# Transposes of the RMS norms' row sums moved to later places in the tensor engine's order at the borders of the MLP

## The chip, the cores and the metric

The kernel runs as one program on one core of a Trainium2 chip. The core has a tensor engine (PE, with its weight loads shown as PEld), a vector engine (DVE), a scalar engine (ACT), GpSimd (POOL) and a queue for transfers (SP). Each takes its own list of instructions in order, and semaphores tell one engine that another is done. The metric is the device time of one execution in microseconds, the median of several.

## The reference, cut to what matters

It is one step of a two-layer model over 1152 tokens (128 of context, 1024 latent), 1024 features wide. Every layer has a token mixer and an MLP, and an RMS norm stands ahead of each:

```
h = rmsnorm(x, P['norm1'][l]) * (1.0 + sc1) + sh1
mix, new_ctx = token_mixer(h, l, P, ctx)
x = x + g1 * mix
h = rmsnorm(x, P['norm2'][l]) * (1.0 + sc2) + sh2
u = jax.nn.relu(h @ P['w_mlp1'][l])
x = x + g2 * ((u * u) @ P['w_mlp2'][l])
```

`rmsnorm` divides each token's features by the root of their mean square.

## The kernel before, in words

**Layout.** Features lie on the 128 partitions and tokens along the free dimension. `x` is eight tiles (features 0 to 127, 128 to 255 and so on), written x0 to x7 below; the tokens are cut into three blocks of 384 (`tb` 0, 1, 2). Weights and activations are split into a high and a low part (`wh` and `wl`, `hh` and `hl`), and a product takes three matmuls of 128x384.

**The order.** The tensor engine's instructions stand exactly as the Python code issues them. For the other engines a scheduler makes the order when the program is built. Work that is to lie between matmuls is written as generators in `self.chain`; each call of `tick()` advances the first of them by one `yield`. In the MLP and in the input projections a tick comes after every 12 matmuls, in the output projection after every two steps of 6. I call 12 matmuls into one PSUM tile a group.

**A norm of one block** has these steps. `squares` (L305 to L311) squares the eight tiles on ACT and adds them up on DVE or POOL, ending in L311. After some empty ticks `rstd` transposes the sum on the tensor engine (L318, three transposes), reduces it over the features on DVE (L320, L321) and takes the power -1/2 on POOL (L323). `spread` copies the result to a full tile on DVE (L336), and one tick later transposes it back on the tensor engine (L341) and copies it out of PSUM on ACT (L343). Then `norm` makes `hh` and `hl` of the eight tiles, two to a tick: for most of them DVE multiplies (L355), ACT rounds (L356) and DVE takes the rest (L357), for the others POOL multiplies (L359), ACT scales and rounds (L361, L362) and DVE takes the rest (L363). All of these transposes use the one PSUM buffer of `pe`; L508 in the mixer, a transpose of a projection's result copied out by L510 on DVE, uses it too.

**Three borders.** The first is that between the output projection and the MLP of layer 0 (`norm2`), the third the same in layer 1. The output projection works on one block at a time, a group per tile of x, with two PSUM buffers (`pd`); each group is added to x on DVE (L1232) and so gives its buffer free. The weights of two groups come together, with a cast on ACT (L124) and a subtraction on DVE or POOL (L125). `chain` then holds the norms of the three blocks, and the first two row blocks of the MLP's first matrix (`up_unit`, 24 matmuls each) are made for block 0, then for block 1, then for block 2. What they leave is squared on ACT and POOL (L1266 to L1268) and split on DVE (L1269). The second border is that between the MLP of layer 0 and the projections of layer 1 (`norm1`): the last piece of the second matrix (`down_chunk`, added to x by L1290) is made block by block, with the norm of each block behind it.

## Time and profile before

| | us |
|---|---|
| median of 3 runs | 2906.37 (2906.33 to 2909.56) |
| the profiled execution's own time | 2915.1 |
| its span, first to last instruction | 2913.3 |
| busy in it: PE, DVE, ACT, POOL | 2750.3, 1457.1, 1119.5, 796.9 |

The profile is of one execution, whose times are a little longer than the median; differences are taken inside it. An engine's idle time costs something only where another engine, in the end the tensor engine, waits for it.

### The profile page before, as it was taken

The page shows a single profiled execution, that of the slowest core. Times are in us where ns is not written, and L with a number is a line of the kernel's source. Part 1 is how long each engine was busy: PE and PEld are TensorE (multiplying, and loading weights), DVE is VectorE, ACT ScalarE, POOL GpSimd, SP SyncE. Part 2 cuts the span into 40 slices and gives each one's busy share as a digit, 9 for nine tenths or more (in the row PEclk, how much of TensorE's full clock was granted, in tenths as well). Part 3 has the DMA queues.
Part 4 walks back from the last instruction along what each step waited for, and adds up shares of the span by engine and source line. Part 5 has one row for each costly group of instructions (what it writes and reads, how often), then busy time and mean ns, then how long its engine had stood idle before and what let it go on. Part 6 is the DMA issues. An engine that isn't in the chain of part 4 may idle for free. (4 is left out here: it accounts for less than half of the span.)

```text
span 2913.3 us, 41546 instructions
## 1 busy us (share of the span) xinstructions
PE 2750.3 (94%) x16067; PEld 2626.7 (90%) x16067; DVE 1457.1 (50%) x2577; ACT 1119.5 (38%) x2046; POOL 796.9 (27%) x848
## 2 busy tenths in 40 slices
PE   5898889999999999999988989899899999999998
PEld 4887887889999999999977879878899999999998
DVE  7645677795332333233475547868832333233235
ACT  4645447764112112211356436477622112211223
POOL 4233446642001001100223244576311001100112
PEclk7999999999999999999999999999999999999999
DMA  7545348321221111111343643662211111111113
GB/s 262 136 124 158 97 150 259 122 80 58 94 84 40 44 44 44 39 42 44 111 114 91 174 126 102 209 206 79 67 43 44 44 44 37 44 44 44 43 38 130
DMA packets 279301, 273.64 MB, mean 94 GB/s; under 512 B 30032, under 2 KB 259008, under 8 KB 279104
## 3 DMA queue, kind: packets, MB, share of 16 engines
q1 hardware_dynamic: 278888, 270.92, 30.5%
q8 instruction: 127, 2.08, 0.3%
q14 instruction: 70, 0.57, 0.1%
q10 hardware_dynamic: 216, 0.06, 0.0%
HBM read 227.02 MB, written 43.91 MB: 93 GB/s over the span
## 5 line engine op out<-in xcount | busy, mean ns | idle before, releaser
L161 PE MATMUL pg<-hh,wh 128*128 128x384 f32 x1856 | 634.6, 342 | 1.8 <-ACT hh L356 1.8
L162 PE MATMUL pg<-hl,wh 128*128 128x384 f32 x1856 | 630.3, 340 | 3.1 <-DVE hl L363 1.6
L163 PE MATMUL pg<-hh,wl 128*128 128x384 f32 x1856 | 629.5, 339 | 0.0
L124 ACT CAST wh<-wr 128x1024 fp32r<-128x1024 f32 x228 | 239.0, 1048 | 914.3 <-PE pg L162 878.7
L1268 POOL TENSOR_TENSOR te<-te 128x384 f32<-128x384 f32 x192 | 166.1, 865 | 1331.3 <-ACT uh L1267 1331.0
L163 PE MATMUL pg<-uh,wl 128*128 128x384 f32 x1536 | 514.1, 335 | 1.7 <-DVE wl L125 1.7
L161 PE MATMUL pg<-uh,wh 128*128 128x384 f32 x1536 | 515.0, 335 | 0.6 <-ACT wh L124 0.6
L162 PE MATMUL pg<-ul,wh 128*128 128x384 f32 x1536 | 513.8, 335 | 0.0
L1290 DVE SCALAR_TENSOR_TENSOR x<-pg,mod,x 128x384 f32<-128x384 f32 (+2 forms) x512 | 254.2, 515 | 395.7 <-PE pg L163 395.6
L161 PEld LDWEIGHTS pg<-hh,wh 128*128 128x128 f32 x1856 | 350.6, 189 | 8.6 <-issue 5.0
L162 PEld LDWEIGHTS pg<-hl,wh 128*128 128x128 f32 x1856 | 350.8, 189 | 6.1 <-DVE hl L363 3.1
L125 DVE TENSOR_TENSOR wl<-wr,wh 128x1024 fp32r<-128x1024 f32 x196 | 244.8, 1249 | 216.3 <-ACT wh L124 216.3
L163 PEld LDWEIGHTS pg<-hh,wl 128*128 128x128 f32 x1856 | 350.3, 189 | 0.0
L1269 DVE TENSOR_TENSOR ul<-te,uh 128x384 fp32r<-128x384 f32 x192 | 107.1, 558 | 452.0 <-POOL te L1268 452.0
L161 PEld LDWEIGHTS pg<-uh,wh 128*128 128x128 f32 x1536 | 288.5, 188 | 4.3 <-issue 1.7
L163 PEld LDWEIGHTS pg<-uh,wl 128*128 128x128 f32 x1536 | 288.5, 188 | 2.3 <-DVE wl L125 2.2
L162 PEld LDWEIGHTS pg<-ul,wh 128*128 128x128 f32 x1536 | 288.5, 188 | 0.0
L1266 ACT ACTIVATE te<-pg 128x384 f32<-128x384 f32 x192 | 93.8, 489 | 358.5 <-PE pg L163 358.5
L161 PE MATMUL pd<-hh,wh 128*128 128x384 f32 x544 | 198.8, 366 | 7.8 <-DVE te L558 3.6
L162 PE MATMUL pd<-hl,wh 128*128 128x384 f32 x544 | 192.2, 353 | 3.4 <-DVE hl L397 3.4
L163 PE MATMUL pd<-hh,wl 128*128 128x384 f32 x544 | 191.4, 352 | 0.0
L1225 PE MATMUL pd<-mh,wh 128*128 128x384 f32 x384 | 137.2, 357 | 13.3 <-DVE x L1232 13.3
(293 smaller groups left out, 4216.4 us busy)
## 6 DMA issues: line engine op xcount, KB each, us to landing
wr<-in_w_mlp_dram SPq DMA_DIRECT2D x144, 512.0 KB, 4.0
wm<-in_w_mod_dram SPq DMA_DIRECT2D x96, 512.0 KB, 4.9
wr<-in_w_out_dram SPq DMA_DIRECT2D x48, 512.0 KB, 4.6
wr<-in_w_in_dram SPq DMA_DIRECT2D x36, 512.0 KB, 5.3
xd<-x SPq DMA_DIRECT2D x48, 192.0 KB, 3.8
x<-xd SPq DMA_DIRECT2D x48, 192.0 KB, 4.3
raw<-mixd SPq DMA_DIRECT2D x40, 192.0 KB, 3.0
B<-gkd SPq DMA_DIRECT2D x16, 288.0 KB, 4.7
```

Of the source, the lines that this page charges most:

```text
L124: nc.scalar.copy(hi[:, :m], raw[:, :m])
L125: lo_eng.tensor_tensor(lo[:, :m], raw[:, :m], f32(hi[:, :m]), ALU.subtract)
L161: mm(out, wh[i], xs[i][0], start=i == 0, stop=False)
L162: mm(out, wh[i], xs[i][1], start=False, stop=False)
L163: mm(out, wl[i], xs[i][0], start=False, stop=i == n - 1)
L1225: nc.tensor.matmul(p[:, :TB], wh[:, k, sl], xs[k][0], start=k == 0, stop=False)
L1266: nc.scalar.activation(r, p[:, :TB], AF.Relu)
L1268: nc.gpsimd.tensor_tensor(r, r, r, ALU.mult)
L1269: nc.vector.tensor_tensor(blk(ul, tb), r, f32(blk(uh, tb)), ALU.subtract)
L1290: nc.vector.scalar_tensor_tensor(xa, p[:, a:b], self.M[l]["g2"][:, dt, s:s + 1], xa, ALU.mult, ALU.add)
```

## The change

It gives `norm_rs` and `spread` a number of empty ticks (`slack`) and sets it by block and border. At the first and third border the spread of block 0 gets one more empty tick, the sum of block 1 one more, and block 2's sum has its squares issued at once, in tiles of the pool `te`, while its transposes queue behind the norm of block 1 and not ahead of the norm of block 0. At the second border block 0's spread gets one more tick, and block 2's sum has four empty ticks and not two. No instruction is added or removed.

```diff
-    def norm_rs(self, x, tb, ret, alloc=None, eng0=None):
+    def norm_rs(self, x, tb, ret, alloc=None, eng0=None, slack=2):
         acc = self.squares(x, tb, alloc, eng0)
-        for _ in range(2):
+        for _ in range(slack):
             yield
         ret[tb] = self.rstd(acc)
         yield
 
-    def spread(self, rs, tile):
+    def spread(self, rs, tile, slack=1):
...
-        for _ in range(1):
+        for _ in range(slack):
             yield
...
-        pbs = yield from self.spread(ret[tb], tile)
+        pbs = yield from self.spread(ret[tb], tile, 1 if tb else 2)
...
-                    self.chain.insert(0, self.norm_rs(self.xa, 1, self.rs2, eng0=nc.vector))
+                    self.chain.insert(0, self.norm_rs(self.xa, 1, self.rs2, eng0=nc.vector, slack=3))
...
-            self.chain.insert(0, self.norm_rs(self.xa, 2, self.rs2, eng0=nc.vector))
+            rs2 = self.norm_rs(self.xa, 2, self.rs2, self.te, nc.vector, slack=1)
+            next(rs2)
+            self.add(rs2)
             norm2(2)
...
-                self.add(self.norm_rs(self.xa, tb, self.rs1))
+                self.add(self.norm_rs(self.xa, tb, self.rs1, slack=2 if tb < 2 else 4))
```

Between the transposes the tensor engine's list has these numbers of other matmuls. First and third border: L318 of block 0, then 24 to its L341 (now 36), 96 to L318 of block 1 (96), 36 to its L341 (48), 60 to L318 of block 2 (48), 24 to its L341 (24); the MLP's first matmul stands 24 behind L341 of block 1 before, and right behind it now. Second border: 24 (now 36), 108 (108), 24 (24), then 72 to L318 of block 2 with L508 among them (84), and 24 to its L341 (none but another L508).

The scheduler moves the other engines' instructions with them. On DVE, at the first border where the norm of block 0 begins (x_3702 to x_3709 are x0 to x7), the difference is this:

```order
 L1232 SCALAR_TENSOR_TENSOR x_3703<-pd,mod_1_2797,x_3703 128x384
 L1232 SCALAR_TENSOR_TENSOR x_3704<-pd,mod_1_2797,x_3704 128x384
+L1232 SCALAR_TENSOR_TENSOR x_3705<-pd,mod_1_2797,x_3705 128x384
 L355 SCALAR_TENSOR_TENSOR tn<-x_3702,G_5516,tn 128x128
 L355 SCALAR_TENSOR_TENSOR tn<-x_3702,G_5516,tn 128x256
```

The addition for x3 has moved ahead of the norm's first multiplication, as the matmuls of x3 have ahead of L341. On ACT the copy L343 stands likewise behind one more L124, and on POOL the multiplications L359 behind one more L125.

On DVE at the same border, where the sum of block 2 is reduced (L320), the list before is this, from the end of its squares (L311):

```order
L311 TENSOR_TENSOR tn<-tn 128x384
L1269 TENSOR_TENSOR ul<-te,uh 128x384
L363 TENSOR_TENSOR hl_6220<-tn,hh_6212 128x384
L320 TENSOR_REDUCE ms<-pe 128x3
L357 SCALAR_TENSOR_TENSOR hl_6221<-tn,mod_1_2797,hh_6213 128x384
```

And now:

```order
L311 TENSOR_TENSOR te<-te 128x384
L363 TENSOR_TENSOR hl_6218<-tn,hh_6210 128x384
L357 SCALAR_TENSOR_TENSOR hl_6219<-tn,mod_1_2797,hh_6211 128x384
L1269 TENSOR_TENSOR ul<-te,uh 128x384
L363 TENSOR_TENSOR hl_6220<-tn,hh_6212 128x384
L357 SCALAR_TENSOR_TENSOR hl_6221<-tn,mod_1_2797,hh_6213 128x384
L355 SCALAR_TENSOR_TENSOR tn<-x_3708,G_5516,tn 128x384
L355 SCALAR_TENSOR_TENSOR tn<-x_3709,G_5516,tn 128x384
L1269 TENSOR_TENSOR ul<-te,uh 128x384
L363 TENSOR_TENSOR hl_6222<-tn,hh_6214 128x384
L357 SCALAR_TENSOR_TENSOR hl_6223<-tn,mod_1_2797,hh_6215 128x384
L357 SCALAR_TENSOR_TENSOR hl_6224<-tn,mod_1_2797,hh_6216 128x384
```

hl_6217 to hl_6224 are the low parts of tiles 0 to 7, here all of block 1, and L320 is the row behind the last of these. Between L311 and L320 stood two instructions, and now stand eleven, up to the end of block 1's norm.

On the tensor engine at the second border, around the transposes of block 2, the difference is this:

```order
 L162 MATMUL pg<-hl_12731,wh 128x384
 L163 MATMUL pg<-hh_12723,wl 128x384
+L318 MATMUL pe<-ident,tn 128x128 x3
+L508 MATMUL pe<-ident,te 128x128 x3
 L341 MATMUL pe<-ident,tn 128x128 x3
-L508 MATMUL pe<-ident,te 128x128 x3
 L161 MATMUL pg<-hh_12716,wh 128x384
```

L318 has come down by 24 matmuls and now stands, with only L508 between, ahead of the L341 that needs its result.

## Rows read from the trace of the kernel before

**Rows 1.** Busy time by stretch (us, busy and count by engine, PE clock, DMA)

```profile
612.50:678.40 65.90, 56.58 (x319) 53.73 (x319) 61.71 (x101) 41.03 (x80) 24.66 (x20) 1.00 0.23 72
678.40:1445.00 766.60, 766.60 (x4401) 757.83 (x4400) 254.38 (x438) 162.94 (x260) 83.13 (x95) 1.00 0.19 58
1445.00:1509.00 64.00, 54.26 (x293) 51.47 (x292) 53.60 (x85) 36.55 (x72) 21.22 (x20) 0.95 0.37 113
2036.90:2102.70 65.80, 58.30 (x313) 55.81 (x313) 60.20 (x100) 40.94 (x80) 24.03 (x20) 0.95 0.24 72
```

**Rows 2.** PE's waits in the first border: total us, times, longest

```profile
PE pe L318 <- DVE tn L311: 4.8, 2, 3.0
PE pd L1225 <- DVE x L1232: 3.4, 2, 1.8
```

**Rows 3.** PE's waits in the second border

```profile
PE pe L318 <- DVE tn L311: 4.0, 2, 3.0
...
PE pg L163 <- DVE wl L125: 1.7, 1, 1.7
...
PE pe L508 <- ACT tn L343: 0.6, 1, 0.6
```

**Rows 4.** PE's waits in the third border

```profile
PE pe L318 <- DVE tn L311: 4.7, 2, 3.0
```

**Rows 5.** PE in order of time, first border: start, us, instruction, [idle before]

```profile
617.21 0.49 PE L341 MATMUL pe<-ident,tn 128*128 128x128 f32 x3
619.51 0.44 PE L1225 MATMUL pd<-mh,wh 128*128 128x384 f32 x1 [1.82 <-DVE x L1232]
...
627.63 0.41 PE L1225 MATMUL pd<-mh,wh 128*128 128x384 f32 x1 [1.60 <-DVE x L1232]
...
660.83 0.52 PE L318 MATMUL pe<-ident,tn 128*128 128x128 f32 x3 [3.01 <-DVE tn L311]
...
665.64 0.52 PE L341 MATMUL pe<-ident,tn 128*128 128x128 f32 x3
```

**Rows 6.** DVE in order of time, first border

```profile
616.51 2.42 DVE L1202 TENSOR_TENSOR ml<-oraw,mh 128x128 fp32r<-128x128 f32 x1
...
619.90 1.66 DVE L355 SCALAR_TENSOR_TENSOR tn<-x,G,tn 128x128 f32<-128x128 f32 x3
...
626.88 0.60 DVE L1232 SCALAR_TENSOR_TENSOR x<-pd,mod,x 128x384 f32<-128x384 f32 x1
...
659.34 1.35 DVE L311 TENSOR_TENSOR tn<-tn 128x384 f32<-128x384 f32 x1
...
662.35 0.55 DVE L320 TENSOR_REDUCE ms<-pe 128x3 f32<-128x384 f32 x1
...
676.78 1.18 DVE L357 SCALAR_TENSOR_TENSOR hl<-tn,mod,hh 128x384 fp32r<-128x384 f32 x1
```

**Rows 7.** POOL in order of time, first border

```profile
616.42 2.36 POOL L125 TENSOR_TENSOR wl<-wr,wh 128x1024 fp32r<-128x1024 f32 x1
618.74 2.01 POOL L359 TENSOR_TENSOR tn<-x,tn 128x384 f32<-128x384 f32 x2
```

**Rows 8.** ACT in order of time, first border

```profile
615.30 1.05 ACT L124 CAST wh<-wr 128x1024 fp32r<-128x1024 f32 x1
617.73 0.48 ACT L343 COPY tn<-pe 128x384 f32<-128x384 f32 x1 [1.39 <-PE pe L341]
```

**Rows 9.** PE in order of time, second border

```profile
1494.15 0.52 PE L318 MATMUL pe<-ident,tn 128*128 128x128 f32 x3 [2.98 <-DVE tn L311]
...
1500.26 0.49 PE L341 MATMUL pe<-ident,tn 128*128 128x128 f32 x3
```

**Rows 10.** DVE in order of time, second border

```profile
1494.70 0.56 DVE L320 TENSOR_REDUCE ms<-pe 128x3 f32<-128x384 f32 x1 [0.70 <-PE pe L318]
...
1496.43 0.55 DVE L336 COPY tn<-rs 128x384 f32<-128x384 f32 x1 [0.97 <-POOL rs L323]
```

**Rows 11.** Busy time by stretch, behind the second border's longest wait

```profile
1495.40:1498.80 3.40, 3.40 (x12) 3.40 (x12) 0.61 (x2) 0.00 (x0) 0.86 (x1) 0.50 0.02 5
```

## The prediction

> **What bounds the kernel now.** I read the busy time by stretch first. In the stretch of the first MLP the tensor engine is busy for all of its 766.6 us, 4401 matmuls at 0.174 us each; the second MLP runs the same code. In the three borders it is not: 9.3 of 65.9 us are idle in the first, 9.7 of 64.0 in the second, 7.5 of 65.8 in the third [rows 1]. Nothing after a border then has slack to take up a delay, so a microsecond won or lost in a border is one in the total. All that this change can win lies in those 26.5 us.
>
> Then the waits, border by border. The transposes of the sums (L318) wait for the end of the squares (L311) on DVE: 4.8 us in two waits in the first border, 4.0 in the second, 4.7 in the third, the longest of each 3.0, which is that of block 2 [rows 2, 3, 4]. The other waits are on DVE as well, or on the scalar engine behind it. DVE itself is busy for 61.7 of the 65.9 us of the first border [rows 1]. The reader should keep this number: the tensor engine waits there because DVE has no time left, and a matmul order that only moves a wait gives DVE none. What helps is only what spares DVE idle time; what costs is what makes it idle.
>
> **The change part by part.** Twelve matmuls take 2.1 us and 24 take 4.2. I go through the first border and sum up what becomes later.
>
> *Block 0's L341 behind one more group.* Before, it ran at 617.21, and then the tensor engine waited 1.82 us, until 619.51, for the addition of x1, which frees a PSUM buffer [rows 5]. That addition is late because a DVE subtraction of 616.51 took 2.42 us, ending as POOL's weight subtraction of 616.42 (2.36 us) ends [rows 6, 7]. Neither is touched, so the third group still cannot start before 619.5. It ends at 621.7; only then L341 runs, outside any wait: 0.4 us that were free. The copy to SBUF (L343, 0.48 us, at 617.73 before) now stands behind a second weight cast of 1.05 us, which waits for the same group since it overwrites its weights [rows 8]: 621.7 + 1.05 + 0.5 gives 623.2. DVE's first multiplication of block 0 was at 619.90 [rows 6], so it is 3.3 us late, and DVE has only the addition for x3 to do meanwhile. From that first multiplication to the addition for x4 DVE took 7.0 us, 619.90 to 626.88 [rows 6], and the next group, at 627.63, waited 1.60 us for it [rows 5]. In the new order four instructions have left this path (x3's addition, two pieces for x4, one low part), estimated at 1.7 us together from three multiplications that took 1.66 us beside POOL [rows 6]. So x4 comes at 623.2 + 7.0 - 1.7 = 628.5 and not 626.9: **1.6 us later**. It could be 0, if the rest of the list gives it back, or 2.5, if POOL's multiplications, two in 2.01 us [rows 7], all fall on DVE's.
>
> This last point is a rule too. The rows show that DVE's subtraction of two SBUF tiles ends only when POOL's does, while additions that read PSUM ran beside POOL. The Trainium skill, "SBUF — State Buffer", section "Who interferes with whom", says that a DVE instruction with two SBUF inputs and a GpSimd instruction that reads SBUF exclude each other for the whole instruction. By the rule alone, with three more POOL multiplications of 1.0 us falling on DVE's in each outer border, the sum below would be 6 us greater; the trace agrees with the lock, but how the two meet in the new order no row shows.
>
> *Block 1's L318, 12 matmuls later.* Its wait was 1.8 us (4.8 less 3.0) [rows 2]; 2.1 us of matmuls now run ahead of it, but the squares inherit part of the delay above. I take **1.2 us won**, between 0.6 and 1.8.
>
> *Block 2's L318, 12 matmuls later, its squares issued at once.* The wait was 3.0 us [rows 5]. DVE now does three instructions of block 1's norm among these squares that it had done before (0.5 us each), with one more POOL multiplication beside them. I take **1.5 us won**, between 0.5 and 3.0.
>
> *Block 2's reduction (L320) behind all of block 1's norm on DVE.* Before, it began 1.7 us after L311's end at 660.7, at 662.35, and L341 followed 3.3 us later, at 665.64 [rows 5, 6]. During that time DVE worked on block 1. Now eleven instructions stand between L311 and L320. At some 0.5 us each and one POOL square of 1.0 us that is 6.6 us. From L320 to the end of the copy L336 it takes 2.3 us at least: 1494.70 to 1496.98, in the second border where nothing stands between [rows 10]. So L341 comes 8.9 us after L311, against 5.0. The tensor engine has L318 and 24 matmuls to do in it, 4.6 us, both before and now. It is kept waiting for the rest, partly by block 1's last low parts, partly by L341 itself, behind which the ready unit of block 1 queues: **4.2 us lost** (2.5 to 5).
>
> *Block 2's norm.* From L341 to its last low part, 665.64 to 677.96, were 12.3 us [rows 5, 6], in which the tensor engine had 36 matmuls and then most of the unit that reads them, 10.6 us: 1.7 late. Now L341 is 24 matmuls ahead, so 8.5 us, and the chain is 11.2, two low parts of block 1 (1.1 us) having gone out of it: 2.7 late, **1.0 us lost** (0 to 2). In this time DVE has also lost cover: while L323, L336, L341 and L343 pass the sum along, it has one low part of the MLP to do.
>
> The first border sums to 1.6 + 0.4 - 1.2 - 1.5 + 4.2 + 1.0 = **4.5 us lost**; as the parts share causes I hold 0 to 7 possible. The third border has the same order and the same two waits at L318 [rows 4]: another **4.5 us**, 0 to 7.
>
> *Second border.* L318 of block 2 moves 24 matmuls down, so its 3.0 us wait goes [rows 3]. But L341 now follows with only L508 between. From L318's start to the copy's end were 2.8 us, 1494.15 to 1496.98 [rows 9, 10]; the single PSUM buffer of `pe` must also be emptied of L508's result first (0.5). Less 0.8 for the two sets of transposes 2.6 us come back. The 24 matmuls took 5.6 us, from 1494.67 to 1500.26 [rows 9], since the engine's clock was granted at half (1.2 GHz) from 1495.4 to 1498.8, after the wait [rows 11]; now they run ahead of any wait, 1.4 us less. I leave a like slow stretch behind the new wait, 1.3 us. L508's 0.6 us behind L341 goes, block 1's 1.0 us at L318 goes, and the weight waits (1.7 at the low part [rows 3]) move on to the next pair of weights, which now stands behind the norm: 0.6 us more. Sum: -3.0 + 2.6 - 1.4 + 1.3 - 0.6 - 1.0 + 0.6 = **1.5 us won**, between 4 won and 1 lost.
>
> Together 4.5 + 4.5 - 1.5 = 7.5 us lost. The profiled execution took 2915.1 us and would take 2922.6; it stands 8.7 us above the median of 2906.4, to which I carry the difference: **2914 us**.
>
> **The rivals.** *The waits at L318 go and nothing comes back* (faster). All of 4.8 + 4.0 + 4.7 = 13.5 us [rows 2, 3, 4] would be won: 2893. Its point is the reduction: if in the outer borders L320 of block 2 runs early enough for L341 to come within the 4.6 us of matmuls behind L318, the 4.2 us term vanishes. For it speaks that L318's are the largest group of waits; against it that L320 stands behind eleven instructions and DVE's list is taken in order. Anything from 2893 to 2900 would be this case.
>
> *It balances* (within 0.2%, which is 5.8 us and about what a measurement of this kernel can tell from no change). If DVE's instructions meet fewer of POOL's than I think, the front costs nothing and the tail 2.5, not 4.2: an outer border then sums to 0 + 0.4 - 1.5 - 2.2 + 2.5 + 1.0 = 0.2, the total to -1, 2905. DVE's work is the same before and after, which speaks for it; the idle time that it gets while the copy is on its way speaks against.
>
> *The clock falls in all borders.* The new waits come close together (the one at x4, block 1's low parts, L341, block 2's low parts). A half-rate stretch like that of 1495.4, in which 12 matmuls began in 3.4 us [rows 11], against 20 at 0.174, costs 1.3 us. Two more in each outer border would give 2914 + 5 = 2919. For it speaks the 0.95 of the second and third border; against it that the first had 9.3 us of waits and kept 1.00 [rows 1], and that a slow tensor engine costs nothing while DVE is late. The Trainium skill, "TensorE: Matmul & The Clock Gate", section "What's actually happening", has the clock halve when the engine has been idle and rise after it has been kept busy; the second border agrees.
>
> **How the numbers follow.** My forecast, 5.8 to 11 us lost, gets 0.43; the clock's case, beyond that, 0.12; balance 0.33; the faster case 0.12. So slower 0.55, same 0.33, faster 0.12. The likeliest's own range is 2912 to 2917. For 8 in 10 I go from 2903, which leaves out the faster case and a little of balance, to 2923, both borders near their upper bound.
>
> **What the profile after would show.** Right: the first border's wait at L318 shrinks from 4.8 to about 3; a wait of about 2 us stands before block 2's L341, where none was; the group after x4's addition starts 1 to 2.5 us later, seen from block 0's L318; L162 waits in the units of blocks 1 and 2 for low parts, some 4 us together; the two outer borders each take about 70 us, not 66; in the second L318 does not wait and L341 does, for 2 to 3 us. Wrong: if L320 of block 2 is not late on DVE, the 4.2 us are wrong; if the outer borders take 66 us or less, so is the sum. The forecast fails as well if DVE's busy time in a border shrinks by several us, because POOL and DVE meet less often than before.

## The result, and the profile after

The change makes the kernel slower: 2923.81 us (median of 4 runs, 2921.97 to 2925.34) against 2907.97 us beside it (2906.33 to 2911.37). The ratio is 1.0053, with an interval of 1.0035 to 1.0070, which is 15.4 us (10 to 20). The direction of the forecast was right and its size was half: 7.5 us. The time lies just above 2923, the upper end of the range that was to hold in 8 cases of 10.

The two profiled executions cannot be compared by their spans (2913.3 and 2921.1 us). Ahead of the first border, where both run the same instructions, the one before lost 6.75 us more. So I measure from one L318 of block 0 to the next. The tensor engine in order of time, before (the last row is the first L318 of the final norm):

```profile
612.62 0.55 PE L318 MATMUL pe<-ident,tn 128*128 128x128 f32 x3
1445.44 0.49 PE L318 MATMUL pe<-ident,tn 128*128 128x128 f32 x3
2037.03 0.44 PE L318 MATMUL pe<-ident,tn 128*128 128x128 f32 x2
2864.20 0.49 PE L318 MATMUL pe<-ident,tn 128*128 128x128 f32 x3
```

And after:

```profile
605.87 0.44 PE L318 MATMUL pe<-ident,tn 128*128 128x128 f32 x2
1445.32 0.49 PE L318 MATMUL pe<-ident,tn 128*128 128x128 f32 x3
2039.14 0.44 PE L318 MATMUL pe<-ident,tn 128*128 128x128 f32 x2
2872.05 0.49 PE L318 MATMUL pe<-ident,tn 128*128 128x128 f32 x3
```

The first border with its MLP took 832.82 us and takes 839.45; the third 827.17 and 832.91. Between them lies a mixer whose length varies, so for the second border I compare matmul by matmul: the 300th behind L318, where the border is over, comes 3.07 us later than before. Busy time by stretch, the three borders after, answering to [rows 1]:

```profile
605.75:678.30 72.55, 60.08 (x319) 56.06 (x319) 62.69 (x101) 41.45 (x80) 23.96 (x20) 0.95 0.22 65
...
1444.90:1511.90 67.00, 56.67 (x296) 53.21 (x294) 55.73 (x87) 37.34 (x72) 24.88 (x23) 0.90 0.36 109
2039.00:2110.60 71.60, 59.44 (x314) 55.39 (x313) 61.82 (x100) 41.36 (x80) 23.95 (x20) 0.95 0.22 66
```

The same 319 matmuls stand in 72.55 us and not 65.90. Of the 6.65 us more, 3.15 are idle time of the tensor engine and 3.50 are busy time (60.08 less 56.58): the granted clock is 0.95 and was 1.00, so some of the same matmuls ran at half rate. DVE's work in the stretch is nearly the same, 62.7 us against 61.7. The waits of the first border, answering to [rows 2]:

```profile
PE pd L1225 <- DVE x L1232: 4.9, 2, 2.7
PE pg L162 <- DVE hl L363: 2.7, 3, 1.2
PE pe L318 <- DVE te L311: 1.8, 1, 1.8
PE pe L341 <- DVE tn L336: 1.7, 1, 1.7
PE pg L162 <- DVE hl L357: 1.4, 2, 0.9
```

L318 lost 3.0 of its 4.8 us, as the change intends. In their place stand 1.7 at L341, 4.1 at low parts (L162), where 1.1 stood, and 1.5 more at x's additions. The second border, answering to [rows 3]:

```profile
PE pg L163 <- DVE wl L125: 4.0, 2, 3.4
PE pg L161 <- ACT hh L356: 2.9, 1, 2.9
PE pe L341 <- DVE te L510: 1.6, 1, 1.6
```

Its 4.0 us at L318 are gone altogether, and 4.0 stand at the weights' low parts, where 1.7 stood, 2.9 at `hh`, where 1.8 stood, and 1.6 at block 2's L341. The tensor engine at the front of the first border, answering to [rows 5]:

```profile
612.75 0.45 PE L1225 MATMUL pd<-mh,wh 128*128 128x384 f32 x1 [2.17 <-DVE x L1232]
616.38 0.62 PE L341 MATMUL pe<-ident,tn 128*128 128x128 f32 x3
623.90 0.66 PE L1225 MATMUL pd<-mh,wh 128*128 128x384 f32 x1 [2.72 <-DVE x L1232]
```

DVE there and at block 2's reduction, answering to [rows 6]:

```profile
616.62 0.62 DVE L1232 SCALAR_TENSOR_TENSOR x<-pd,mod,x 128x384 f32<-128x384 f32 x1 [3.40 <-PE pd L1227]
617.93 4.25 DVE L355 SCALAR_TENSOR_TENSOR tn<-x,G,tn 128x128 f32<-128x128 f32 x3 [0.69 <-ACT tn L343]
...
655.82 1.35 DVE L311 TENSOR_TENSOR te<-te 128x384 f32<-128x384 f32 x1
...
663.89 0.54 DVE L320 TENSOR_REDUCE ms<-pe 128x3 f32<-128x384 f32 x1
```

And POOL at the front, answering to [rows 7]:

```profile
617.47 2.39 POOL L125 TENSOR_TENSOR wl<-wr,wh 128x1024 fp32r<-128x1024 f32 x1 [5.45 <-ACT wh L124]
619.82 2.21 POOL L359 TENSOR_TENSOR tn<-x,tn 128x384 f32<-128x384 f32 x2
```

DVE waits 3.40 us for the tensor engine, which works on the group ahead of L341. Its first three multiplications then take 4.25 us (1.66 before) and end at 622.18, as POOL's do at 622.03. L320 runs 6.7 us behind the end of L311 (663.89 less 657.17), where 6.6 had been worked out.

### The profile page after: what moved, and what is told of

The parts are those of the page before. It is cut to its first block, busy times and chain, and to the rows that moved or that the text cites. A ratio compares the mean times of both kernels' runs of the same rounds, so it can differ in the third digit from the quotient of the medians.

```text
span 2921.1 us, 41549 instructions
## 1 busy us (share of the span) xinstructions
PE 2755.6 (94%) x16067; PEld 2628.1 (90%) x16067; DVE 1458.9 (50%) x2577; ACT 1120.5 (38%) x2046; POOL 798.2 (27%) x848
## 5 line engine op out<-in xcount | busy, mean ns | idle before, releaser
L162 PE MATMUL pg<-hl,wh 128*128 128x384 f32 x1856 | 630.9, 340 | 9.9 <-DVE hl L363 5.9
L124 ACT CAST wh<-wr 128x1024 fp32r<-128x1024 f32 x228 | 239.0, 1048 | 932.0 <-PE pg L162 880.9
L162 PE MATMUL pg<-ul,wh 128*128 128x384 f32 x1536 | 514.1, 335 | 0.0
L162 PEld LDWEIGHTS pg<-hl,wh 128*128 128x128 f32 x1856 | 350.0, 189 | 16.4 <-DVE hl L363 8.9
L125 DVE TENSOR_TENSOR wl<-wr,wh 128x1024 fp32r<-128x1024 f32 x196 | 245.4, 1252 | 219.0 <-ACT wh L124 219.0
L162 PEld LDWEIGHTS pg<-ul,wh 128*128 128x128 f32 x1536 | 289.0, 188 | 0.0
L162 PE MATMUL pd<-hl,wh 128*128 128x384 f32 x544 | 191.8, 353 | 3.4 <-DVE hl L397 3.4
```

What stands on the lines that cost most here:

```text
L124: nc.scalar.copy(hi[:, :m], raw[:, :m])
L125: lo_eng.tensor_tensor(lo[:, :m], raw[:, :m], f32(hi[:, :m]), ALU.subtract)
L162: mm(out, wh[i], xs[i][1], start=False, stop=False)
```

## The experiments

All runs in one table: the ratio to the kernel before; the distance from L318 to L318 for the first and the third border (us); and how much later than before the 300th matmul behind the second border's L318 comes. Where a border's code is unchanged, the traces spread by themselves: 832.8 to 834.7, 826.1 to 827.2, and 0 to 1.7 (mean 1.1). A border's cost is read against the means 833.5, 826.6 and 1.1 of the unchanged ones. What makes the spread is told under "The half-rate stretches".

| kernel | ratio (95%) | first | third | second |
|---|---|---|---|---|
| before | | 832.82 | 827.17 | 0 |
| the change | 1.0053 (1.0035 to 1.0070) | 839.45 | 832.91 | 3.07 |
| 1: block 0's L341 later, outer | 1.0030 (1.0019 to 1.0042) | 837.61 | 830.07 | 1.49 |
| 2: block 1's sum later, outer | 0.9992 (0.9983 to 1.0001) | 832.41 | 825.80 | 0.03 |
| 3: block 2's sum, outer | 1.0022 (1.0013 to 1.0031) | 837.53 | 830.89 | 0.77 |
| 4: block 0's L341 later, second | 1.0013 (1.0004 to 1.0022) | 832.83 | 826.12 | 3.68 |
| 5: block 2's sum later, second | 0.9999 (0.9990 to 1.0009) | 834.73 | 827.11 | 0.07 |
| 4, weights asked for early | 1.0022 (1.0013 to 1.0031) | 833.48 | 826.12 | 5.77 |
| change, block 2's sum inserted | 1.0060 (1.0045 to 1.0075) | 841.15 | 832.31 | 3.01 |
| change, wait filled | 1.0041 (1.0027 to 1.0055) | 838.30 | 833.94 | 3.41 |
| 1 and 4, copy on DVE | 1.0049 (1.0033 to 1.0064) | 836.68 | 831.06 | 4.94 |
| 1 and 4, ticks kept | 1.0055 (1.0042 to 1.0069) | 838.14 | 832.36 | 4.63 |
| 2, wait filled | 0.9993 (0.9985 to 1.0002) | 832.15 | 825.43 | 1.34 |
| 2 in all borders | 0.9997 (0.9988 to 1.0006) | 832.51 | 825.62 | 1.10 |
| before, less on DVE | 0.9972 (0.9959 to 0.9984) | 829.10 | 822.48 | 1.72 |
| change, less on DVE | 1.0034 (1.0021 to 1.0046) | 836.12 | 829.59 | 2.35 |
| before, weights by DVE | 0.9991 (0.9981 to 1.0000) | 831.64 | 824.30 | 1.43 |
| 1, weights by DVE | 1.0014 (1.0004 to 1.0024) | 834.72 | 829.06 | 1.73 |
| change, weights by DVE | 1.0029 (1.0018 to 1.0040) | 833.98 | 828.28 | 3.05 |

### Single parts

Each part of the change alone, on the kernel before. The edits 1 and 4 give `norm` the number of empty ticks, at the outer borders or at the second:

```diff
-        pbs = yield from self.spread(ret[tb], tile)
+        pbs = yield from self.spread(ret[tb], tile, slack)
...
+                                        lambda kt, b: blk(hl[kt], b), slack=1 if tb else 2))
...
+                         lambda kt, b: blk(self.hl1[kt], b), lambda: self.spill(tb), slack=1 if tb else 2)
```

The other edits are lines of the change: 2 `slack=3` for block 1's sum, 3 the three lines of `rs2`, 5 `slack=2 if tb < 2 else 4`.

> One part alone: in the outer borders block 0's L341 stands 12 matmuls later, all else as before. If the front is late because its copy L343 and DVE's first multiplication come later (my term, which measured 3.0 us in the changed kernel), each outer border is 2 to 4 us longer, seen from one L318 of block 0 to the next, and the time 4 to 8 us above the kernel before. If DVE makes good the delay before the sum of block 1 is wanted, the wait at block 1's L318 shrinks and the time is within 2 us of before. If it is the clock that made the front dear, the border is longer by 1.3 us for each half-rate stretch that appears and by no more.

> One part alone: in the outer borders block 1's L318 stands 12 matmuls later. Before, it waited 1.8 us for DVE and block 2's L318 waited 3.0. My term has 1.2 us won per outer border, 2.4 in all. If DVE alone sets the time, the wait is only handed on: none is left at block 1's L318, that of block 2 grows to 4 to 5 us, and the time is within 1 us of before. If the waits of the sums are a cost by themselves, 3.6 us are won.

> One part alone: in the outer borders block 2's squares are issued at once and its L318 queues behind the norm of block 1. My terms: 1.5 us won at L318, 4.2 lost because L320 stands behind block 1's norm on DVE, 1.0 lost in block 2's own norm, so 3.7 per outer border and 7.4 in all. If the wait at L318 goes and nothing comes back, 3 us are won per border. If the front and not the tail carries the loss, it is within 2 us of before.

> One part alone: in the second border block 0's L341 stands 12 matmuls later. In the changed kernel the first wait for the low part of the weights (L163 behind L125) was 3.4 us where 1.7 and 0.6 had been forecast together, and a half-rate stretch of 6.8 us stood around it. If this part puts L125 on DVE behind more of the norm, the wait is 2.5 to 3.5 us here too and the second border 1.5 to 4 us longer. If the later place of block 2's sum does it, the wait stays at 1.7 and the border within 0.5 us.

> One part alone: in the second border the sum of block 2 has four empty ticks and not two, so that L318 stands 24 matmuls later and L341 right behind it. My terms: the 3.0 us at L318 go, 2.6 come back at L508 and L341, 1.4 us of half-rate matmuls go, 1.3 come again behind the new wait, L508's 0.6 go: 1.1 us won. If the waits at L508, L341 and the first matmul of block 2's projection together come to more than the 3.0 + 0.6 + 1.8 us that stood there before, this part wins nothing, and the other three parts explain the whole change. The first weight wait stays at 1.7 us by either.

Part 1 costs 4.1 us in the first border and 3.5 in the third, 8.7 in all by the ratio. In the third border no half-rate stretch fell (clock 1.00 over its 66.8 us), and it shows the mechanism clean: against the unchanged third border at clock 1.00 (826.12 us, twice) it costs 4.0 us. The tensor engine there:

```profile
2033.23 0.55 PE L318 MATMUL pe<-ident,tn 128*128 128x128 f32 x3
...
2042.34 0.49 PE L341 MATMUL pe<-ident,tn 128*128 128x128 f32 x3
2049.98 0.41 PE L1225 MATMUL pd<-mh,wh 128*128 128x384 f32 x1 [2.98 <-DVE x L1232]
2063.53 0.52 PE L318 MATMUL pe<-ident,tn 128*128 128x128 f32 x3 [2.77 <-DVE tn L311]
2084.10 0.52 PE L318 MATMUL pe<-ident,tn 128*128 128x128 f32 x3 [2.95 <-DVE tn L311]
```

The group behind x4's addition comes 16.75 us behind L318, where it came 15.01 behind it before (627.63 [rows 5] less 612.62): 1.74 later, against a forecast of 1.6. But block 1's L318 then waits 2.77 us, 1 us more than its 1.8 [rows 2], and block 2's again 2.95 as in [rows 5]. The delay is handed through to the end and grows on the way. DVE's idle time shows it: of the 48.06 us from block 0's L318 to the end of block 2's squares DVE was busy for 44.85 before, and here for 43.69 of 50.72. It has 7.0 us idle and not 3.2, with less work, not more.

Part 2 wins all of block 1's 1.8 us at L318, and by the end of the border about 1.0 is left. Part 3 costs 4.0 and 4.3 us, near the 3.7 forecast. Part 5 is at 1.0 us won by its trace and 0.3 by its ratio (1.1 forecast): less than the spread of the unchanged traces, and its ratio's interval cannot tell it from nothing. Part 4 costs 2.6 us by its trace and 3.8 by its ratio, and the first weight wait is the 3.41 us of the change, so the later L341 makes it and not the place of block 2's sum. The five ratios sum to 16.3 us, the change has 15.4, which their intervals (some 3 us either way for each) cannot tell apart. By the traces the three parts of an outer border sum to 7.0 us, and the change has 6.0 and 6.3.

### The second border: do the weights make the loss?

```diff
+            early = len(tbs) == 1 and l == 0
+            w = prep(0) if early else None
             for dp in range(KD // 2):
-                wh, wl = self.load_w(I["w_mlp2"][l, c * CH * 128:(c + 1) * CH * 128, dp * 256:dp * 256 + 256]
...
+                wh, wl = w if early else prep(dp)
+                if early and dp + 1 < KD // 2:
+                    w = prep(dp + 1)
```

> The second border's part alone, as in the run before with L341 of block 0 12 matmuls later, but the weights of each pair in the last piece of layer 0's second matrix are asked for one pair ahead, so that their subtraction L125 stands earlier among the norm's instructions on DVE (five places before, to one behind the first group's). If the part costs 2.5 to 3.8 us because the weights' low part comes late on DVE, the wait of 3.4 us goes and the second border is 2 to 4 us shorter than with the part alone, 590 to 592 us. If the norm itself is late for what reads it, the wait is found again at the squares' L318 or at low parts, and the border stays at 593 to 595.

The wait moved and the loss stayed. The tensor engine in that border:

```profile
1458.73 0.45 PE L163 MATMUL pg<-uh,wl 128*128 128x384 f32 x1 [1.34 <-DVE wl L125]
...
1473.80 0.88 PE L318 MATMUL pe<-ident,tn 128*128 128x128 f32 x3 [4.74 <-DVE tn L311]
```

With the weights late, block 1's L318 did not wait; with the weights early it waits 4.74 us. The 144th matmul, just behind it, comes 2.50 us later than before in the one and 2.54 in the other. So the norm's start on DVE is what is late, and the weights only showed it first. The border's end is no better (5.77 against 3.68).

### The tail: does the place of block 2's sum matter?

```diff
             next(rs2)
-            self.add(rs2)
+            self.chain.insert(0, rs2)
```

> The changed kernel, but in the outer borders block 2's sum is put back ahead of the norms of block 0 and 1 in the chain, its squares still issued at once: L318 stands 12 matmuls behind block 1's L341 and 48 ahead of its own L341 (48 and 24 in the changed kernel). Then L320 no longer stands behind block 1's norm on DVE. If that place makes the 1.7 us at L341 and part of the low parts' waits, they go, but L318 waits for its squares again, 3 to 6 us, since 36 fewer matmuls stand ahead of it: the time is 2 to 6 us above the changed kernel. If L318's waits are made by too few matmuls alone and L341's by its place, the two balance and the time is within 2 us of the changed kernel.

Nothing was won. All the waits of the change's tail (7.6 us in seven of them) became one. The tensor engine:

```profile
656.48 0.87 PE L318 MATMUL pe<-ident,te 128*128 128x128 f32 x3 [8.06 <-DVE te L311]
```

The squares end 51.2 us behind block 0's L318 (656.32 less 605.09), in the change 51.3 (657.17 less 605.87). The order of the tensor engine's list decides where it waits for DVE, here not how long.

### The half-rate stretches

In the first border of the change the clock was granted at half (1.2 GHz) from about the end of each of the two first waits (2.17 and 2.72 us):

```profile
613.20:616.60 3.40, 3.40 (x13) 3.31 (x13) 0.02 (x1) 0.26 (x1) 0.00 (x0) 0.50 0.50 159
623.50:626.90 3.40, 3.00 (x9) 3.03 (x10) 3.30 (x9) 3.24 (x8) 0.00 (x0) 0.50 0.00 0
```

In two runs a wait is filled with transposes that nothing reads:

```diff
+                if k in (4,):
+                    f = self.pg()
+                    for _ in range(18):
+                        nc.tensor.transpose(f[:, :128], self.ident, self.ident)
...
+        if fill:
+            f = self.pg()
+            for _ in range(fill):
+                self.nc.tensor.transpose(f[:, :128], self.ident, self.ident)
         ret[tb] = self.rstd(acc)
```

> The changed kernel with 18 more transposes of a constant in each outer border, into a PSUM buffer that nothing reads, ahead of the group that waits for x's addition 6.9 us behind block 0's L318 (2.2 us there). They take 2.0 us of that wait; DVE's, ACT's and POOL's lists stay the same. If the half-rate stretch that followed the wait in the changed kernel made the front dear, the stretch goes, block 0's L341 comes 9.1 us behind L318 and not 10.5, and each outer border is about 1.4 us shorter. If DVE's lateness made it dear, L341 may come earlier, but block 1's L318 comes 32 us behind as before. If the transposes last longer than the wait, the border is longer by the rest.

> Block 1's sum 12 matmuls later in the outer borders, as in the run of that part alone, with 11 transposes of a constant (1.2 us) ahead of block 2's L318, where the tensor engine waits 2.95 us; the other engines' lists stay the same. With the part alone 1.8 us were won at block 1's L318, and 1.5 of them went to a half-rate stretch behind block 2's L318. If the wait brought that stretch, a shorter one does not, and each outer border is 1.8 us shorter than before and not 0.3: 4 us under the kernel before in all. If 1.75 us of waiting are enough to bring it, or it comes elsewhere, the time stays where the part alone had it, 2 to 3 under.

In the change the fill did what it should in the first border. The first stretch is gone, and L341 comes 9.1 us behind L318, not 10.5:

```profile
607.75 0.55 PE L318 MATMUL pe<-ident,tn 128*128 128x128 f32 x3
616.84 0.49 PE L341 MATMUL pe<-ident,tn 128*128 128x128 f32 x3
624.48 0.41 PE L1225 MATMUL pd<-mh,wh 128*128 128x384 f32 x1 [2.98 <-DVE x L1232]
```

The border is 1.15 us shorter. In the third a half-rate stretch of 6.8 us came behind the next wait instead, with another near the border's end, and it is 1.0 longer. The ratio, 1.0041, is not told apart from 1.0053. So this stretch costs 1.2 us, by one trace, where DVE waits for the group that it slows.

On part 2 the answer is another. Behind block 2's L318 the clock was 0.53 with the part alone (first row) and 1.00 with the fill (second row, the other run):

```profile
651.28:654.68 3.40, 3.40 (x12) 3.40 (x13) 3.40 (x7) 1.32 (x2) 1.83 (x2) 0.53 0.00 0
```

```profile
651.63:655.03 3.40, 3.40 (x21) 3.40 (x22) 3.40 (x7) 1.41 (x3) 1.83 (x2) 1.00 0.00 0
```

The 1.8 us won are still there 24 matmuls behind L318, and then go all the same, in the run with the fill to a wait for low parts (whose lines L363 and L357 are L367 and L361 there):

```profile
657.88 0.44 PE L162 MATMUL pg<-hl,wh 128*128 128x384 f32 x1 [0.30 <-DVE hl L367]
659.63 0.44 PE L162 MATMUL pg<-hl,wh 128*128 128x384 f32 x1 [0.95 <-DVE hl L361]
```

The first border is 832.15 and not 832.41: this half-rate stretch had cost 0.3 us, since the tensor engine would have waited for DVE.

What the stretches of the change cost is shown best by a run made for something else. Up to block 1's L318, the run with block 2's sum inserted has the change's instructions in the change's order on every engine, the same in its first border (first row) as in its third (second row):

```profile
605.09:637.12 32.03, 27.25 (x139) 26.34 (x139) 26.09 (x44) 17.11 (x34) 9.39 (x7) 0.89 0.25 82
2040.78:2070.58 29.80, 24.45 (x140) 23.37 (x139) 25.99 (x44) 17.30 (x34) 9.38 (x7) 1.00 0.26 87
```

In both the tensor engine waits twice for x's additions (2.16 and 2.63 us; 2.17 and 2.99). In the first border the clock was granted at half (1.2 GHz) from about the end of each wait, in the third it stayed at 2.4 GHz, and the first is 2.2 us longer. Both outer borders of the profiled change are like the first: two such stretches, and 32.04 and 32.21 us.

The unchanged borders say the same. The first border in the kernel before, in part 4 with early weights, and in part 5, each from L318 over 319 matmuls:

```profile
612.62:678.40 65.78, 56.46 (x319) 53.73 (x319) 61.59 (x100) 41.03 (x80) 24.66 (x20) 1.00 0.23 72
608.13:674.60 66.47, 57.76 (x319) 55.28 (x319) 61.61 (x100) 40.69 (x80) 24.79 (x20) 0.97 0.23 71
603.89:671.60 67.71, 59.03 (x319) 56.55 (x319) 61.68 (x100) 40.69 (x80) 24.77 (x20) 0.95 0.23 70
```

From L318 to L318 these take 832.82, 833.48 and 834.73 us, and part 4 alone, again at 1.00, takes 832.83. The third border takes 826.12 twice at 1.00, and 827.17 and 827.11 at 0.95. So the spread of the unchanged borders is the clock, and one half-rate stretch in them costs 0.5 to 1 us. Against the unchanged borders at 1.00 the change costs 6.6 and 6.8 us, some 2.2 of them, at the price of the two rows above, by its two stretches. In the second border the unchanged traces are 0 at a clock of 0.95, 0.8 and 1.3 at 0.92, and 1.4 to 1.7 at 0.90; the change had 0.90, and its 3.07 are 1.5 more than that. Whole executions point the same way: the mean clock is 0.9745 in the four of the change and 0.9759 in 106 of the kernel before.

### What is late at the front

Three runs look for what delays DVE behind the later L341: the copy L343 made by DVE, the chain's later steps kept at their ticks, and part 2 taken to the second border too.

```diff
+        pbs = yield from self.spread(ret[tb], tile, slack, nc.vector.tensor_copy if slack > 1 else None)
...
-            if kt < 7 and (tb < 2 or kt % 2):
+            if kt < 7 and (tb < 2 or kt % 2) and not (slack > 1 and kt == 0):
...
+                self.add(self.norm_rs(self.xa, tb, self.rs1, slack=3 if tb == 1 else 2))
```

> Block 0's L341 12 matmuls later in all three borders, as in the two runs of one part (together 12.5 us above the kernel before), but the copy of its result out of PSUM (L343) is made by DVE and not by ACT, where it stood behind a second weight cast of 1.05 us. If that cast is a part of the delay, the group after x4's addition comes 0.5 to 1 us later than before and not 1.75, and the time is 2 to 4 us lower than the two parts together, 8 to 10 above before. If the later matmuls alone make it, nothing is won, and DVE's own 0.5 us for each copy come on top: 12 to 14 above before.

> Block 0's L341 12 matmuls later in all three borders, but the first two pieces of its norm are issued in one tick, so that all that stands behind them in the chain keeps its tick: block 1's L341 comes back to 36 matmuls behind its L318 in the outer borders (48 with the part alone), and block 1's L318 in the second border to its old place. If the part alone was dear because it moved every later step of the chain by 12 matmuls as well, the wait of 1.8 us for block 1's low parts goes, an outer border is 2 to 3 us above before and not 4, and the second border loses less than 2.5. If only the late start of DVE counts, the outer borders stay at 4 and the second at 2.5 to 3.7.

> Block 1's sum 12 matmuls later in all three borders, and nothing else of the change. In the second border block 1's L318 waited 1.0 us before. If what the outer borders showed holds there, that wait goes and is not handed on to block 2's L318, since the tensor engine's next steps also hand DVE its work earlier: 1.0 us won there and 3 in all under the kernel before. If DVE alone sets the end, block 2's L318 waits 1.0 longer and the second border stays at 590 to 592 us.

None of them wins. With the copy on DVE the first multiplications start earlier and end no earlier, 15.0 us behind L318 in both (part 1: 616.42 + 4.24 less 605.66; here 617.32 + 4.59 less 606.92). So the scalar engine's cast, a part of my 3.3 us, was not the limit. With the ticks kept the wait for block 1's low parts goes, and block 1's L318 comes 4.6 us later than before instead of 3.6. In the second border block 1's wait of 1.0 at L318 is won (the 132nd matmul comes 1.4 earlier) and goes back at its own L341, which waits 0.80 us for L336, and at block 2's L318, which waits 3.34 us where it waited 2.98.

What the first multiplications end with is POOL. DVE in part 1 alone:

```profile
616.42 4.24 DVE L355 SCALAR_TENSOR_TENSOR tn<-x,G,tn 128x128 f32<-128x128 f32 x3 [0.83 <-ACT tn L343]
```

And POOL beside it:

```profile
615.96 2.39 POOL L125 TENSOR_TENSOR wl<-wr,wh 128x1024 fp32r<-128x1024 f32 x1 [4.14 <-ACT wh L124]
618.29 2.22 POOL L359 TENSOR_TENSOR tn<-x,tn 128x384 f32<-128x384 f32 x2
```

Three runs give block 1's weights to DVE:

```diff
-                               .rearrange("(k p) c -> p k c", p=128), 4, nc.vector if (tb, half) in ((0, 1), (2, 0)) else nc.gpsimd)
+                               .rearrange("(k p) c -> p k c", p=128), 4, nc.vector if (tb, half) in ((0, 1), (1, 0), (2, 0)) else nc.gpsimd)
```

> The kernel before, with the low parts of block 1's weights in the second half of the output projection (L125, 2.4 us each on POOL, 1.2 on DVE) made by DVE and not by POOL. It is the reference for the next run. DVE gets 1.2 us more for each of the two that fall into the border, POOL's two are gone: the outer borders are between 2 us longer and 1 us shorter.

> Block 0's L341 12 matmuls later in the outer borders, on top of that kernel. With the weights on POOL, DVE's first three multiplications of block 0 took 4.2 us in all behind the later L341 (1.7 before), and ended with POOL's subtraction and multiplications; the border was 3.9 us longer. If DVE's multiplications of two SBUF tiles were held by POOL's subtraction, they take 2.5 us or less here, and an outer border is at most 2 us longer than in the run beside it without the later L341. If they are late for another reason, the difference stays at 3 to 5 us per border.

> The changed kernel with the same weights' low parts made by DVE. If POOL's subtraction is a part of its front's loss, its outer borders lose 1 to 3 us less against the run without the change than the 5.7 to 6.8 us of the changed kernel; the tail (block 2's L320 behind block 1's norm) keeps its 4 us. If it is not, the difference stays at 6 to 7 us per border.

DVE in part 1 with that edit: two multiplications 2.26 us, and the third 0.34.

```profile
616.79 2.26 DVE L355 SCALAR_TENSOR_TENSOR tn<-x,G,tn 128x128 f32<-128x128 f32 x2
...
619.76 0.34 DVE L355 SCALAR_TENSOR_TENSOR tn<-x,G,tn 128x128 f32<-128x128 f32 x1
```

So POOL's subtraction had held them, and the loss of 1.7 us at x4's group is gone: that group comes 1.2 us earlier than in the run without part 1. The border follows only in part. The tensor engine now waits 1.69 us for the weights' low part (L1227), which the edit itself put on DVE. Block 1's L318 is 1.1 us late, and behind it the clock was at half:

```profile
635.10:638.50 3.40, 3.40 (x12) 3.40 (x12) 2.56 (x7) 0.79 (x2) 0.89 (x1) 0.50 0.43 129
```

The run without part 1 began 21 matmuls in the same place in 3.4 us, at 1.00. So the 144th matmul is 2.7 us late, and the two borders cost 3.1 and 4.8 us. The 3.1 are the cleaner figure: in the third the run without part 1 had its full clock and this one 0.92. In the whole change the edit does better. The outer borders lose 2.3 and 4.0 us to the run beside it, not 6.0 and 6.3, and the ratios differ by 11.1 us, not 15.4. But this run had no half-rate stretch ahead of block 1's L318 in either border, where the change had two worth 2.2 us. So how much of the 2 to 4 us is POOL's subtraction itself, and how much the stretches that were not there, the runs do not show.

### Less work on DVE

```diff
-                    eng.tensor_tensor(acc, acc, sq, ALU.add)
+                    if eng0 is None or kt == 4 * h + 1:
+                        eng.tensor_tensor(acc, acc, sq, ALU.add)
```

> The kernel before with less work on DVE: in the outer borders the sums of blocks 1 and 2 add up only two of the four squares of each half, so the squares of four tiles are left out of each of these sums and four of DVE's additions (0.54 us each) go out of each. If DVE's amount of work bounds the border, the waits at L318 (4.8 us) shrink by 3 us or more and each outer border is 2 to 4.5 us shorter: 5 to 9 us under the kernel before. If the waits come from how far an order of single steps reaches, and not from the amount, they stay above 3.5 us and less than 2 us are won in all.

> The changed kernel with the same additions left out. If its loss comes from idle time given to a DVE that has none to spare, DVE catches up here: the outer borders lose 2 to 4 us to the other kernel with less work, not 6.6, and the two kernels differ by 7 to 11 us, not 15.8. If the loss stands in the tensor engine's order alone (the half-rate stretches, the places of L341), the two differ by 14 to 17 us as with all the work.

The first is 8.1 us faster by its ratio and L318 waits no more: DVE's work does set the borders before. The second misses: the two differ by 18 us, and by 7.0 and 7.1 per outer border, no less than with all the work. Matmul by matmul, the front of the first border is 1.7 us late at x4's group and 1.4 at the 240th; then come 2.6 and 2.7 us, all in the tail, at low parts and in matmuls at half rate (clock 0.50 from 658.5 to 661.9). With L318's waits gone before, there is nothing left for the tail to win, and its whole cost shows. That DVE's want of slack alone makes the loss is refuted: the tail is a matter of the order.

## Why the prediction was wrong, point by point

**Block 2's sum in the outer borders: right as a sum.** -1.5 + 4.2 + 1.0 = 3.7 us per border; part 3 alone measures 4.0 and 4.3, with another split: all 3.0 us at L318 go, and L341 waits 2.6. In the change L320 runs 6.7 us behind L311 for 6.6 forecast, L341 waits 1.67 us, and L162 waits 4.1 in all for "some 4".

**Block 1's L318: right in size when alone.** 1.2 us were forecast and about 1.0 is measured. The wait is won whole (1.8), and the rest goes back at low parts. So in the change L318's waits in the first border shrink to 1.8 us, further than to the "about 3" of the forecast.

**The front: two errors that cancel.** The prediction read "x4 comes 1.6 us later" plus 0.4, and closed there. The 1.6 was right (1.74), but the step priced the delay where it is felt first. DVE's first multiplication is 3.5 us later (10.75 us behind L318, 7.28 before) and DVE has little idle time in which to make that good, so the delay comes again at block 1's L318 and at its low parts: part 1 alone costs 4.0 us at full clock and not 2.0. In the change, though, block 1's L318 stands 12 matmuls later and takes back more than the 1.2. At full clock (third border with block 2's sum inserted) it comes 29.80 us behind block 0's L318; 27.5 before and 2.1 for the 12 matmuls make 29.6. So 0.2 us were lost by there, where 1.6 + 0.4 - 1.2 = 0.8 had been forecast: near, and by luck.

**The clock: the step that failed in the outer borders.** The prediction put half-rate stretches there at nothing, because "a slow tensor engine costs nothing while DVE is late". Ahead of L341 and of x's next groups it is DVE that waits for the tensor engine, and two stretches stand there in each outer border of the change. They cost 2.2 us (32.03 against 29.80 for the same instructions). Against the unchanged borders at full clock the outer borders cost 6.6 and 6.8 us; without the 2.2 they are at 4.4 and 4.6, and 4.5 was forecast. Against the mean of the unchanged borders, which have half-rate stretches of their own, they cost 6.0 and 6.3.

**The rule that was set aside.** The Trainium skill, "SBUF — State Buffer", section "Who interferes with whom", has a DVE instruction with two SBUF inputs and a GpSimd instruction that reads SBUF exclude each other. The trace agrees: 4.25 us for three multiplications that end with POOL's, 2.6 with the subtraction gone. By the rule alone my sum would have been 6 us greater, 13.5, near the 15.4 measured, but not for its reason. It had supposed three of POOL's multiplications; in the trace one weight subtraction, which the later L341 had put beside DVE's first instructions, held the first of DVE's multiplications, and two of POOL's multiplications the others. That made 2.6 us more on DVE (4.25 less 1.66), of which at full clock 0.2 us are left at block 1's later L318.

**The second border: the other step that failed.** Its sum was -1.5 us; measured against the unchanged traces it is +2.0 (3.07 less 1.1), or +1.5 against those of the same clock. The terms of block 2 (-3.0 + 2.6 - 1.4 + 1.3 - 0.6) are not contradicted as a sum: -1.1 forecast, -1.0 by part 5's trace, -0.3 by its ratio. L341 waits 1.6 us there, of the 2 to 3 forecast. What failed is "the weight waits move on: 0.6 us more" and "block 1's 1.0 us at L318 goes". I had priced the later L341 of block 0 as a wait handed on, not as a later start of DVE. Part 4 measures +2.6 by its trace and +3.8 by its ratio, not -0.4, and the run with early weights shows that it is the same 2.5 us whichever instruction waits.

Together: 2 x 4.5 - 1.5 = 7.5 us were forecast; 6.0 + 6.3 + 2.0 = 14.3 are read from the traces, and 15.4 from the ratio. The error of some 7 is 3.3 in the outer borders, which is about what their half-rate stretches cost beyond those of the unchanged borders, and 3.5 in the second border.

**The rivals.** "Nothing comes back" needed L320 to be early and is refuted by its place. "It balances" supposed a front that costs nothing, which at full clock is nearly so (0.2 us), and a cheaper tail, which part 3 refutes (4.0 and 4.3 us). "The clock falls in all borders" was right that stretches come (two in each outer border) and nearly right in their price (2.6 us forecast for two, 2.2 measured). It is about half of what the forecast missed; the second border is the rest. The price depends on the place: 1.2 us ahead of DVE's start, 0.3 in part 2 where the tensor engine waits for DVE.

**What stays open.** Why the stretches fall into the fronts of the change, and in what share of its executions, no run shows: the profiled one had them in both outer borders, and the run with block 2's sum inserted in one of two. With POOL's subtraction gone part 1 still costs 3.1 us, of which 1.1 at block 1's L318 and some 1.6 in half-rate matmuls behind it are read from the trace; that DVE's late start makes the first is argued. No version beats the kernel before beyond doubt: part 2 alone and the weights by DVE are at 0.9992 and 0.9991, with intervals that reach 1.0001 and 1.0000.

## What to carry to other kernels

Where a second engine is busy for nearly the whole of a stretch, price a move by when that engine starts and by its idle time, not by the first wait that it changes: a start 3.5 us late, alone, cost 1.7 us at the next wait and 4 in the end. Read the granted clock of a stretch before two traces of it are compared: here the same border took 832.8 or 834.7 us by its half-rate stretches, and the changed front 29.8 or 32.0. A wait that goes is not a gain until the next instruction that needs the same engine has been looked at; the wait of 4.7 us at L318 behind a weight wait that had gone is the plainest case. And read what a third engine does at the place of the move: POOL's subtraction, which no line of the change names, came to lie on DVE's first multiplications.

## What the runs showed of the hardware that was not expected

Three small multiplications on DVE with two SBUF tiles took 4.24 us beside a POOL subtraction of 2.39 us and two POOL multiplications of 2.22 us together, and one took 0.34 us with POOL idle. Each ended 0.15 to 0.3 us behind one of POOL's three instructions (at 618.50, 619.66 and 620.66 in part 1, POOL's at 618.35, 619.38 and 620.51): that is as if the two engines took turns, one whole instruction each, and DVE's short ones lasted about as long as POOL's. Where half-rate stretches fall is not fixed by the order of the instructions: in one execution of part 1, whose two outer borders run the same list, one fell into the first and none into the third, and with block 2's sum inserted two fell into the first front and none into the third, behind nearly the same waits.
